# Pinning the high parts and squares of x tiles and of later tables on ScalarE, a later norm spread, and another product order for the last pair

## The chip, the cores and the metric

The kernel runs on one core of one Trainium2 chip. The metric is the device time of one execution in microseconds (us), lower being better; a measured time is the median of several runs. TensorE multiplies, ScalarE and VectorE work on its results and on its operands, GpSimd (POOL) and SyncE (SP) mostly issue DMAs.

## The reference

One decoder layer over x of shape (1, 2048, 1024) in float32, with 256 memory tokens:

```python
h = rmsnorm(x, mix_norm_g); proj = h @ w_in
q, k, v, g, u = split(proj)                    # five blocks of 512 columns
y_ret  = silu(g) * head_rmsnorm(retention(q, k, v, positions), ret_gn_g)   # 4 heads, rotary, chunks of 128
y_pool = pool_mixer(u, pool_w, pool_scale)     # windows 2, 4, 8, 16: mean minus token, a linear map per group
x = x + concat(y_ret, y_pool) @ w_out
x = x + cross_attn(rmsnorm(x, xa_norm_g), rmsnorm(mem, mem_norm_g), xa_wq, xa_wkv, xa_wo)   # 4 heads of 256
x = x + conv_glu_ffn(rmsnorm(x, ffn_norm_g), ...)   # causal width-3 convolution, silu(gate) * value, D_FF = 2816
return rmsnorm(x, final_norm_g)
```

## The kernel before

All activations stand transposed, channels on the 128 partitions and tokens along the free axis. The sequence is worked on in two halves of 1024 tokens (`b` = 0 and 1, `T` = 1024), each in two sub-halves of 512 (`SUB`). Every product is made of three passes with split operands: `split` writes a high part `hi` (ScalarE, L258, or L261 when a norm weight is multiplied in) and a low part `lo` = value minus `hi` (VectorE, L242 or L250), and `passes` issues hi x hi, hi x lo, lo x hi on TensorE (L266 to L268), 128x128 against 128x512. So almost every operand of TensorE is preceded by one ScalarE and one VectorE instruction.

The stages are: weights folded for the attention and x of the first half loaded (`folded_weights`, `load_x_wide`); for each half the values (`values`), the projections and retention, the output product with residual (`add_residual`), the cross-attention in folded form, and its output product; then the up and the down projections for both halves in `run`, with the sums of a Strassen-like scheme. GpSimd adds up sums of weight blocks in DRAM beside the first half (`weight_sums`), paced by a small ScalarE copy (L1027) and a GpSimd copy.

`attention(sums, beside, pace)` goes over 16 products of a 128-token row tile against a folded table, eight for the first pair of heads (`hp` = 0) and eight for the second (`hp` = 1). Each product is 24 matmuls. Behind it come row maximum, exponentials (ScalarE, L969), normalisation (VectorE, L246), and two products later the transposes of the probabilities (`turn`, TensorE L942, evacuated at L944). `load_m(hp)` fetches a table from DRAM (`Md`) in four pieces and splits it. The table of `hp` = 1 is fetched and split in the first four of the 16 steps.

After the attention of the first half come eight output units, one for each 128 channels (`unit` with `VWd`): 48 matmuls each, evacuated by `add_residual` onto `acc` with the square of the sum (L405 or L409), then stored (L2049). After each unit the program calls `load_x(n, nxt, got)`, which splits channel tile n of the second half of x into `X` and squares it for its norm, and then issues the fetch of the next one (`fetch_x`, L578). `X` is read by the attention's products until those end; the squares read only the fetched tile.

The generator `norms` then makes the factor of the second half's norm (`rows_norm`, narrow matmuls at L347), spreads it over the partitions (`spread_steps`: VectorE writes diagonals, TensorE multiplies them by ones at L398, ScalarE evacuates at L400), and makes the factor of the first half's own norm. It is advanced once for every 12 matmuls of `values`. Beside it `quarter_sums` combines x for the second half's projections (L1577, L1592 and VectorE), in program order already.

`head_projections` does the second half's projections as eight pairs of column blocks (`PAIRS`), each pair with seven products of 12 matmuls each on sums of the operands. Blocks 0 to 3 are q, 4 to 7 k, 8 to 11 the gates, 12 to 15 the pool groups of windows 2, 4, 8, 16. A block is complete when both of its sub-halves were evacuated the last time; a complete pool block queues `pool_steps` on VectorE, a complete q and k pair starts the head's retention (`kept`). Within the last pair these steps are queued behind the last head's factors (`chained`). `settle` splits finished parts into the operands of the output product, whose second half takes the parts in the order 2, 4, 5, 3 (4 is window 2, 5 is window 4). `scaled_tables` reads the rotary tables back from DRAM (`rope_d`) and multiplies them by the spread norm.

The order of the instructions on each engine is not that of the program. The kernel is written with

```python
with tile.TileContext(nc, schedule_with_timeline_sim=True) as tc:
```

and a planner places each instruction into its engine's queue by its own model of when the operands will be there; the queue is then run in that order. Three means set bounds to it: `tc.keep_in_program_order(ins)` puts an instruction behind the one that stands before it in the program on the same engine (and only behind that one); `tc.issue_after(ins)` puts the instructions of a block behind a given one on its engine; `tc.manual_schedule` fixes a stretch.

Of the kernel before, what the change touches and what calls it, by code (L numbers as in the profile page):

```python
# [11 lines left out]
AF = mybir.ActivationFunctionType  # L12
# [9 lines left out]
SUB = 512  # L22
# [8 lines left out]
EDGE = 16  # L31

ROUNDS = ((0, 3), (6, 4), (14, 4))
PAIRS = ((15, 8), (0, 4), (14, 9), (1, 5), (10, 11), (2, 6), (3, 7), (13, 12))

_PI = 314159265358979323846264338327950288419716939937510582097494459
_PI_DEN = 10**62
# [99 lines left out]
def trunk(ctx, tc, xT, memT, pos, w_qkgu, w_v, wkv, wqT, wo, wout_r, wout_p, poolT, w_up, w_dn, vecs, consts, outT):  # L137
    nc = tc.nc
    pe, act, dve, pool, sp = nc.tensor, nc.scalar, nc.vector, nc.gpsimd, nc.sync
# [37 lines left out]
    def vec(n):  # L177
        nonlocal o
        o += n
        return vc[:, o - n : o]  # L180

    mixg, xag, memg, ffng, fing = (vec(KT) for _ in range(5))
# [7 lines left out]
    def cst(n):  # L190
        nonlocal o
        o += n
        return cs_t[:, o - n : o]

    ident, one = cst(P), cst(1)
# [10 lines left out]
    Ud = drp.tile([NF, 4, P, SUB], F32, tag="Ud", name="Ud")  # L206
    Ad = drp.tile([len(PAIRS), 4, P, SUB], F32, tag="Ad", name="Ad")
    Dd = drp.tile([len(ROUNDS), KT // 2, 4, P, SUB], F32, tag="Dd", name="Dd")
# [23 lines left out]
    def aux():  # L232
        if both[0] and next(turns_) % 3 == 2:
            return single()
        return auxp.tile([P, SUB], F32, tag="aux", name=nm("aux"))

    def small(n=4):
        t = smp.tile([P, 8], F32, tag="sm", name=nm("sm"))
        return t[:, :n]

    def tt(eng, out, a, b, op):
        return eng.tensor_tensor(out=out, in0=a, in1=b, op=op)  # L242
# [6 lines left out]
    def stt(out, a, s, b, op0=ALU.mult, op1=ALU.add):  # L249
        dve.scalar_tensor_tensor(out=out, in0=a, scalar=s, in1=b, op0=op0, op1=op1)  # L250

    def bcast(v, n):
        return v.rearrange("p (a o) -> p a o", o=1).to_broadcast([P, v.shape[1], n])

    def split(src, hi, lo, g=None):

        if g is None:
            act.activation(hi, src, AF.Copy)  # L258
            tt(dve, lo, src, hi.bitcast(F32), ALU.subtract)
        else:  # L260
            act.activation(hi, src, AF.Identity, scale=g)  # L261
            stt(lo, src, g, hi.bitcast(F32), ALU.mult, ALU.subtract)

    def passes(ps, lhs, rhs, start, stop, more=False):
        (lh, ll), (rh, rl) = lhs, rhs
        pe.matmul(ps, lh, rh, start=start, stop=False, skip_group_check=more)  # L266
        pe.matmul(ps, lh, rl, start=False, stop=False, skip_group_check=more)  # L267
        latest[0] = pe.matmul(ps, ll, rh, start=False, stop=stop, skip_group_check=more)  # L268

    def new_raw():  # L270
        r = raws.take()
        r.free()
        return r.f
# [6 lines left out]
    def pairs(raw):  # L280

        out = []
        for h in range(2):
            r = raw[h] if isinstance(raw, list) else raw[:, h * SUB : (h + 1) * SUB]
            pr = new_pair()
            split(r, pr[:, 0], pr[:, 1])
            out.append(pr)
        return out
# [10 lines left out]
    def xpair(k, s):  # L299
        return X[:, 2 * k, s * SUB : (s + 1) * SUB], X[:, 2 * k + 1, s * SUB : (s + 1) * SUB]  # L300
# [79 lines left out]
    def spread_steps(y, outs):  # L380

        yh = smp.tile([P, 8], F32R, tag="yh", name=nm("yh"), bufs=1)[:, : y.shape[1]]
        yl = small(y.shape[1])
        dve.tensor_copy(yh, y)
        tt(dve, yl, y, yh.bitcast(F32), ALU.subtract)
        n, ds = SUB // P, []
        for s in range(len(outs)):
            ds.append(prs.take())
            for i, v in enumerate((yh.bitcast(F32), yl)):
                di = ds[s].r[:, i * SUB : (i + 1) * SUB]  # L390
                tt(dve, di.rearrange("p (a b) -> p a b", a=n), ident.rearrange("p (o b) -> p o b", o=1).to_broadcast([P, n, P]), bcast(v[:, s * n : (s + 1) * n], P), ALU.mult)
        yield
        yield
        for out, d in zip(outs, ds):
            ps = aux()
            with tc.issue_after(latest[0].ins):
                for i in range(2):
                    pe.matmul(ps, ones, d.r[:, i * SUB : (i + 1) * SUB], start=i == 0, stop=i == 1)  # L398
            d.free()
            act.activation(out, ps, AF.Copy)  # L400

    def squares(k, src, s_ap, eng=dve):

        if k == 0:
            act.activation(s_ap, src, AF.Square)  # L405
        else:
            q = TT.take()
            m = src.shape[-1]
            act.activation(q.f[:, :m], src, AF.Square)  # L409
            tt(eng, s_ap, s_ap, q.f[:, :m], ALU.add)  # L410
            q.free()


    def folded_weights():
# [166 lines left out]
    def load_x(k, s_acc, got):  # L581

        for s in range(NS):
            r = got[s].f[:, :SUB]
            split(r, *xpair(k, s), mixg[:, k : k + 1])
            squares(k, r, s_acc[s].f[:, :SUB])
            got[s].free()

    def load_x_wide(k, room):
# [324 lines left out]
    def attention(sums, beside, pace):  # L914
# [7 lines left out]
        def load_m(hp):  # L922

            out = mw[hp]
            for kp in range(KT // 2):
                raw = new_raw()
                fetched[0] = sp.dma_start(raw.rearrange("p (k n) -> p k n", k=2), Md[hp, 2 * kp : 2 * kp + 2].rearrange("k p n -> p k n"))
                if hp == 0 and kp == 0:

                    out += [(pr[:, 0], pr[:, 1]) for pr in pairs(raw)]  # L930
                    yield
                    continue
                for i in range(2):
                    u = tables[2 * hp].r[:, (2 * kp + i) * T : (2 * kp + i + 1) * T]
                    split(raw[:, i * SUB : (i + 1) * SUB], u[:, :SUB], u[:, SUB:])
                    out.append((u[:, :SUB], u[:, SUB:]))
                yield

# [11 lines left out]
        for _ in load_m(0):  # L950
            pass
        more_m = load_m(1)
        late = []
        for i in range(2 * KT):
            hp, t = divmod(i, KT)
# [4 lines left out]
            if i == 0:  # L960
                rn, _, _ = norm_tables(sums, wide=False)
# [35 lines left out]
    def weight_sums():  # L997

        jobs = [((w_qkgu[a], w_qkgu[c]), 0, 4, Ad[p]) for p, (a, c) in enumerate(PAIRS)]
        jobs += [((w_up[f], w_up[f + NF]), 0, 4, Ud[f]) for f in range(NF)]  # L1000
# [594 lines left out]
    def head_projections(b, v, rb, t1, t2, z):  # L1595
# [76 lines left out]
        class Heads(Member):  # L1672

            def __init__(self, p):
                super().__init__([w_qkgu[n] for n in PAIRS[p]], Ad[p], 0, 4)
                self.groups, self.how, self.seen, self.acc = PAIRS[p], [""] * 7, set(), None
                self.ended = []
# [87 lines left out]
            ready.append((h, outs[h]))  # L1765

        members = [Heads(p) for p in range(len(PAIRS))]
        items = [(m, i) for m in members for i in range(7)]
        fetches, made, highs = list(items), [], []

        def fetch():
# [147 lines left out]
    for b in range(NB):  # L1919
# [47 lines left out]
        if b:  # L1967
            first, order = 3, (6, 7, 0, 1, 2, 4, 5, 3)
            weights, evacs = [], []
            for n in range(first):  # L1970
                raw = new_raw()
                r = raw.rearrange("p (k c) -> p k c", c=P)
# [12 lines left out]
        for n in range(first, KT):  # L1985
            raw = new_raw()
# [215 lines left out]
```

## Time and profile before

| | |
|---|---|
| median of 3 runs | 2483.67 us (2480.16 to 2487.25) |
| profiled execution | 2483.87 us, span 2482.1 us |
| granted TensorE clock, mean | 0.993 |
| TensorE busy | 2418.8 us (97%) |
| VectorE busy | 1726.2 us (70%) |
| ScalarE busy | 1290.9 us (52%) |
| GpSimd busy | 319.5 us (13%) |
| read from and written to HBM | 398.65 MB, 187.43 MB |

Times inside the execution are in us from the start of its span. In a timeline a row is: start, duration, engine, source line, operation, destination <- sources by the program's names (buffer numbers left out), shape, count, and in brackets the idle time of the engine before it with what ended it. A line such as L242 is that of a helper, so the tile names tell the operations apart: `T` are temporaries, `Q`, `G`, `E`, `S`, `Z` operand buffers, `mm` and `aux` PSUM banks, `sm` small columns. "SPq" and "ACTq" are DMA issues from the queues of SyncE and ScalarE.

### The profile page before, as it was taken

What the parts mean: (1) busy time and instruction counts of PE and PEld (TensorE: products, weight loads), DVE (VectorE), ACT (ScalarE), POOL (GpSimd) and SP (SyncE); (2) the same over time, 40 slices, a digit from 0 to 9 for tenths busy, and PEclk for the clock granted to TensorE, in tenths of its full rate; (3) what the DMA queues carried; (4) which work ended last, traced back from release to release, by engine and by line L of the source; (5) the groups of instructions that cost most, each with busy time, mean ns of one, the idle gap of its engine ahead of it and who ended that gap; (6) DMA issues with size and microseconds to landing.
All of it is one profiled execution on the core that took longest, in us unless ns stands there. A gap on an engine that the chain in (4) does not pass through costs nothing.

```text
span 2482.1 us, 33252 instructions
## 1 busy us (share of the span) xinstructions
PE 2418.8 (97%) x11294; PEld 2018.0 (81%) x11294; DVE 1726.2 (70%) x2917; ACT 1290.9 (52%) x2349; POOL 319.5 (13%) x485
## 2 busy tenths in 40 slices
PE   6999999999999999999999999999999999999997
PEld 6888888877878887788888888888888887888886
DVE  8646576654666765575678876897667687867876
ACT  6333423443435553434655565665555576666663
POOL 1000000044255554200000010020000000000000
PEclk9999999999999999999999999999999999999998
DMA  7133524479799999757468665665456468758951
GB/s 285 50 111 111 159 75 136 140 192 324 211 299 267 278 225 318 204 187 253 146 195 274 215 189 159 219 219 170 160 157 216 134 225 294 248 187 280 344 173 68
DMA packets 263595, 502.35 MB, mean 202 GB/s; under 512 B 28800, under 2 KB 57600, under 8 KB 263424
## 3 DMA queue, kind: packets, MB, share of 16 engines
q1 hardware_dynamic: 201536, 385.90, 47.4%
q0 software_dynamic: 37376, 86.00, 14.7%
q10 hardware_dynamic: 24512, 28.32, 3.3%
q8 instruction: 89, 1.46, 0.2%
q14 instruction: 82, 0.67, 0.1%
HBM read 398.65 MB, written 187.43 MB: 236 GB/s over the span
## 4 chain that ended last, share of the span: by engine, by line
PE 87%; DMA 6%; DVE 4%; ACT 1%; issue 1%; SPq 0%; POOLq 0%; POOL 0%; DVEq 0%; ACTq 0%
PE mm L268 27%; PE mm L266 27%; PE mm L267 27%; DMA T<-xT 2%; DVE Z L242 1%; DMA S<-Md 1%; DVE G L242 1%; DMA rope_d<-T 1%; PE aux L820 1%; PE aux L793 1%; PE aux L804 1%; DVE T L242 1%; PE aux L266 1%; DVE Q L242 1%; PE aux L267 1%
## 5 line engine op out<-in xcount | busy, mean ns | idle before, releaser
L266 PE MATMUL mm<-G,Q 128*128 128x512 f32 (+1 forms) x1745 | 672.3, 386 | 17.3 <-ACT Q L258 11.5
L268 PE MATMUL mm<-G,Q 128*128 128x512 f32 (+1 forms) x1745 | 668.7, 385 | 13.3 <-DVE Q L242 13.2
L267 PE MATMUL mm<-G,Q 128*128 128x512 f32 (+1 forms) x1617 | 619.9, 384 | 0.0
L267 PE MATMUL mm<-G,E 128*128 128x512 f32 x1084 | 421.7, 389 | 0.0
L266 PE MATMUL mm<-G,E 128*128 128x512 f32 x1084 | 420.2, 390 | 0.0
L268 PE MATMUL mm<-G,E 128*128 128x512 f32 x1084 | 419.2, 389 | 0.0
L266 PEld LDWEIGHTS mm<-G,Q 128*128 128x128 f32 x1745 | 331.5, 190 | 82.4 <-ACT Q L258 13.0
L268 PEld LDWEIGHTS mm<-G,Q 128*128 128x128 f32 x1745 | 330.9, 190 | 79.1 <-DVE Q L242 16.1
L267 PEld LDWEIGHTS mm<-G,Q 128*128 128x128 f32 x1617 | 307.2, 190 | 56.4
L242 DVE TENSOR_TENSOR Z<-Z,mm 128x512 f32<-128x512 f32 x296 | 201.9, 683 | 105.5 <-PE mm L268 103.0
L250 DVE SCALAR_TENSOR_TENSOR Z<-Z,vecs 128x1024 f32<-128x1024 f32 x176 | 224.7, 1280 | 50.0 <-ACT Z L1177 45.4
L267 PEld LDWEIGHTS mm<-G,E 128*128 128x128 f32 x1084 | 203.5, 188 | 42.5 <-DVE G L242 0.4
L266 PEld LDWEIGHTS mm<-G,E 128*128 128x128 f32 x1084 | 203.4, 188 | 42.6 <-ACT G L1063 0.4
L268 PEld LDWEIGHTS mm<-G,E 128*128 128x128 f32 x1084 | 203.4, 188 | 42.4
L1114 ACT ACTIVATE E<-R 128x512 fp32r<-128x512 f32 (+1 forms) x165 | 101.5, 615 | 141.0 <-PE mm L267 132.1
L242 DVE TENSOR_TENSOR T<-T 128x512 f32<-128x512 f32 (+3 forms) x220 | 150.6, 690 | 21.3 <-ACT T L409 12.5
L242 DVE TENSOR_TENSOR Q<-R,Q 128x512 fp32r<-128x512 f32 x149 | 103.7, 699 | 77.2 <-ACT Q L258 54.9
L242 DVE TENSOR_TENSOR G<-T,G 128x512 fp32r<-128x512 f32 (+1 forms) x181 | 119.5, 675 | 43.7 <-ACT G L1063 32.0
L1114 ACT ACTIVATE Q<-R 128x512 fp32r<-128x512 f32 (+1 forms) x153 | 94.6, 618 | 87.1 <-PE mm L267 70.9
L1177 ACT ACTIVATE Z<-Z,vecs 128x1024 f32<-128x1024 f32 x88 | 109.1, 1241 | 37.6 <-DVE Z L242 36.7
L1063 ACT ACTIVATE G<-T 128x512 fp32r<-128x512 f32 x157 | 95.6, 624 | 54.7 <-DMA T<-Hd 27.2
L1114 ACT ACTIVATE E<-S 128x512 fp32r<-128x512 f32 (+1 forms) x107 | 65.8, 615 | 104.9 <-PE mm L267 101.3
(338 smaller groups left out, 3783.2 us busy)
## 6 DMA issues: line engine op xcount, KB each, us to landing
T<-Gd SPq DMA_DIRECT2D x168, 256.0 KB, 4.6
Ud<-w_up POOLq DMA_DIRECT2D x132, 256.0 KB, 10.3
Gd<-Z SPq DMA_DIRECT2D x110, 256.0 KB, 2.8
R<-Ud SPq DMA_DIRECT2D x106, 256.0 KB, 2.7
R<-w_up SPq DMA_DIRECT2D x80, 256.0 KB, 3.1
S<-Ud SPq DMA_DIRECT2D x70, 256.0 KB, 2.9
Gd<-T SPq DMA_DIRECT2D x56, 256.0 KB, 3.4
T<-Xd SPq DMA_DIRECT2D x53, 256.0 KB, 4.6
```

The costliest lines, as they stand in the source:

```text
L242: return eng.tensor_tensor(out=out, in0=a, in1=b, op=op)
L250: dve.scalar_tensor_tensor(out=out, in0=a, scalar=s, in1=b, op0=op0, op1=op1)
L266: pe.matmul(ps, lh, rh, start=start, stop=False, skip_group_check=more)
L267: pe.matmul(ps, lh, rl, start=False, stop=False, skip_group_check=more)
L268: latest[0] = pe.matmul(ps, ll, rh, start=False, stop=stop, skip_group_check=more)
L793: pe.matmul(col(sc, c), self.ch(k, c), self.ch(q, c), start=True, stop=True)
L804: pe.matmul(col(self.kv, c), col(self.kn.f, c), self.ch(v, c, h * T), start=True, stop=True)
L820: pe.matmul(col(y, c), col(self.pr.f, c), self.ch(v, c, h * T), start=True, stop=self.cur[c] is None)
L1063: act.activation(hi, x, AF.Copy)
L1114: act.activation(p2[:, 0, :w], self.raw[i].f[:, :w], AF.Copy)
L1177: act.activation(self.c[g].f, a[:, 2:], AF.Identity, bias=cb[:, f : f + 1], scale=cw[2][:, f : f + 1])
```

## The change

Four things are changed. `split` and `squares` take a flag `kept` with which their ScalarE instruction is put behind the previous ScalarE instruction of the program. It is set for the x tiles of the second half in `load_x` (all four ScalarE instructions of a tile) and in `load_m` for the table of the second pair of heads (`hp == 1`), in both halves. `spread_steps` gives control back six times instead of twice between writing the diagonals and multiplying them. In the last pair of column blocks the two blocks change places, (12, 13) for (13, 12), and its seven products run in the order 0, 2, 4, 6, 1, 3, 5.

```diff
-PAIRS = ((15, 8), (0, 4), (14, 9), (1, 5), (10, 11), (2, 6), (3, 7), (13, 12))
+PAIRS = ((15, 8), (0, 4), (14, 9), (1, 5), (10, 11), (2, 6), (3, 7), (12, 13))
...
-    def split(src, hi, lo, g=None):
+    def split(src, hi, lo, g=None, kept=False):
 
         if g is None:
-            act.activation(hi, src, AF.Copy)
+            one = act.activation(hi, src, AF.Copy)
             tt(dve, lo, src, hi.bitcast(F32), ALU.subtract)
         else:
-            act.activation(hi, src, AF.Identity, scale=g)
+            one = act.activation(hi, src, AF.Identity, scale=g)
             stt(lo, src, g, hi.bitcast(F32), ALU.mult, ALU.subtract)
+        if kept:
+            tc.keep_in_program_order(one)
...
-        yield
-        yield
+        for _ in range(6):
+            yield
...
-    def squares(k, src, s_ap, eng=dve):
+    def squares(k, src, s_ap, eng=dve, kept=False):
 
         if k == 0:
-            act.activation(s_ap, src, AF.Square)
+            one = act.activation(s_ap, src, AF.Square)
         else:
             q = TT.take()
             m = src.shape[-1]
-            act.activation(q.f[:, :m], src, AF.Square)
+            one = act.activation(q.f[:, :m], src, AF.Square)
             tt(eng, s_ap, s_ap, q.f[:, :m], ALU.add)
             q.free()
+        if kept:
+            tc.keep_in_program_order(one)
...
-            split(r, *xpair(k, s), mixg[:, k : k + 1])
-            squares(k, r, s_acc[s].f[:, :SUB])
+            split(r, *xpair(k, s), mixg[:, k : k + 1], kept=True)
+            squares(k, r, s_acc[s].f[:, :SUB], kept=True)
...
-                    split(raw[:, i * SUB : (i + 1) * SUB], u[:, :SUB], u[:, SUB:])
+                    split(raw[:, i * SUB : (i + 1) * SUB], u[:, :SUB], u[:, SUB:], kept=hp == 1)
...
-        items = [(m, i) for m in members for i in range(7)]
+        items = [(m, i) for m in members for i in ((0, 2, 4, 6, 1, 3, 5) if m is members[-1] else range(7))]
```

## The prediction

> **What bounds the kernel now.** I read the page first, then busy time by stretches, then the timelines of TensorE, ScalarE, VectorE and SyncE around every hole in TensorE's work.
>
> ```profile
> span 2482.1 us, 33252 instructions
> PE 2418.8 (97%) x11294; PEld 2018.0 (81%) x11294; DVE 1726.2 (70%) x2917; ACT 1290.9 (52%) x2349; POOL 319.5 (13%) x485
> ```
>
> TensorE is busy in 2418.8 of 2482.1 us. The profiled execution took 2483.9 us, 1.8 us over its span and 0.2 us over the median of the three runs (2483.7), so a sum made on its rows can be set against the median as it stands. No engine can save work here, because the change takes no matmul away; what it can win lies in the 63 us in which TensorE stood. The largest part of those lies in the first stage and at the end, which the change doesn't touch. The other holes lie in a few stretches:
>
> ```profile
> 505.00:545.00 40.00, 36.66 (x174) 30.03 (x173) 19.31 (x48) 18.35 (x42) 21.00 (x37) 1.00 0.86 217
> 545.00:590.00 45.00, 40.80 (x188) 33.45 (x187) 21.13 (x47) 17.08 (x47) 23.64 (x38) 0.96 1.07 276
> 590.00:664.00 74.00, 74.00 (x328) 61.28 (x327) 41.59 (x64) 32.56 (x55) 15.87 (x24) 1.00 0.88 268
> 664.00:735.00 71.00, 65.93 (x299) 54.32 (x298) 43.51 (x93) 28.80 (x55) 37.07 (x58) 0.98 1.01 277
> 900.00:960.00 60.00, 52.40 (x262) 42.43 (x261) 36.58 (x79) 22.45 (x59) 30.34 (x44) 0.97 0.90 238
> 1005.00:1040.00 35.00, 31.36 (x150) 25.88 (x150) 18.88 (x52) 12.96 (x31) 7.92 (x11) 1.00 0.97 249
> ```
>
> The columns are length, busy time (instructions) of TensorE, its weight loads, VectorE, ScalarE and GpSimd, the granted clock, the DMA share and GB/s. The stretch 590 to 664 shows TensorE without a hole: 74.00 us for 328 matmuls, 0.226 us each, which is the pace that I use below. The stretches beside it lost 3.34, 4.20, 5.07, 7.60 and 3.64 us, and three of them show a granted clock under 1.00. The first, second and last are the attention of the first and second half of the sequence. The timeline of ScalarE tells why, first for the first half:
>
> ```profile
> ...
> 530.62 0.63 ACT L405 ACTIVATE T<-T 128x512 f32<-128x512 f32 x1 [6.39 <-DMA T<-xT]
> 537.51 0.63 ACT L405 ACTIVATE T<-T 128x512 f32<-128x512 f32 x1 [6.26 <-DMA T<-xT]
> 538.61 0.56 ACT L969 ACTIVATE T<-mm,sm,scl 128x256 f32<-128x256 f32 x1
> ...
> 580.67 0.72 ACT L261 ACTIVATE G<-T,vecs 128x512 fp32r<-128x512 f32 x1 [4.28 <-DMA T<-xT]
> 581.81 0.55 ACT L969 ACTIVATE T<-mm,sm,scl 128x256 f32<-128x256 f32 x1
> ```
>
> L405 and L261 are the square and the high part of an x tile of the next half. They have nothing to do with the attention that runs here. The planner queued them ahead of the exponentials (L969), and ScalarE waited 6.39, 6.26 and, after a like wait, 4.28 us for their tiles, with the exponentials behind them. TensorE runs on until it needs the probabilities to transpose (L942):
>
> ```profile
> ...
> 540.54 0.63 PE L942 MATMUL aux<-consts,T 128*128 128x128 f32 x4 [3.34 <-DVE T L246]
> ...
> 583.73 1.09 PE L942 MATMUL aux<-consts,T 128*128 128x128 f32 x4 [4.20 <-DVE T L246]
> 584.47 0.78 PE L266 MATMUL mm<-G,Q 128*128 128x512 f32 x1
> ...
> 586.93 0.39 PE L266 MATMUL mm<-G,Q 128*128 128x512 f32 x1
> ```
>
> It stands 3.34 us and 4.20 us. After the second hole six matmuls, from 584.47 to 586.93, take 2.46 us in place of 6 x 0.226 = 1.36: another 1.1 us at the lower clock. For the second half the same thing is done by the high parts of the later table:
>
> ```profile
> ...
> 1017.18 1.15 ACT L258 ACTIVATE Z<-S 128x512 fp32r<-128x512 f32 x2 [5.55 <-DMA S<-Md]
> 1023.72 1.16 ACT L258 ACTIVATE Z<-S 128x512 fp32r<-128x512 f32 x2 [5.39 <-DMA S<-Md]
> 1029.10 1.28 ACT L969 ACT_TABLE_LOAD   x1 [4.22 <-DVE sm L246]
> ```
>
> ```profile
> ...
> 1025.60 0.16 DVE L247 TENSOR_SCALAR sm<-aux 128x8 f32<-128x8 f32 x1
> ```
>
> ```profile
> ...
> 1006.65 0.39 PE L266 MATMUL mm<-Q,G 128*128 128x512 f32 x1
> ...
> 1032.24 0.59 PE L942 MATMUL aux<-consts,T 128*128 128x128 f32 x3 [3.64 <-DVE T L246]
> ```
>
> The two Z<-S lines are the later table's, and wait 5.55 and 5.39 us for its DMA. VectorE's low parts follow them in its queue, so the sums of squares are taken up only at 1025.60, the first exponential's table load starts at 1029.10, and TensorE stands 3.64 us at 1032.24.
>
> **The change, part by part.** First, the pinned x tiles. Each high part and square is put behind ScalarE's previous instruction in the program, for the first of a tile the store of the finished residual (L2049). That store needs the output products of the same column tile, so no x tile can come before the attention's exponentials any more. This takes away both holes: 3.34 + 4.20 + 1.1 = 8.6 us. The instructions are the same ones, so nothing is added. The tile's DMA issues are not pinned, though the slots that they fill now come free later. What is late next is the exponentials' own chain. The stretches 505 to 545 and 545 to 590 lost 3.34 and 4.20 us in all, which is these two holes, so nothing else was late there, and I take nothing back.
>
> Where the tiles go now, they have cover if they have landed. An output unit is 48 matmuls, 48 x 0.226 = 10.8 us, and the fetch of the next tile is issued when the squares of one unit release their buffers:
>
> ```profile
> ...
> 631.89 3.66 SPq L578 DMA_DIRECT2D T<-xT  x2
> ```
>
> ```profile
> ...
> 642.18 0.72 ACT L261 ACTIVATE G<-T,vecs 128x512 fp32r<-128x512 f32 x1 [1.67 <-DMA T<-xT]
> ...
> 664.04 0.71 ACT L261 ACTIVATE G<-T,vecs 128x512 fp32r<-128x512 f32 x1
> ...
> 668.43 0.33 ACTq L2049 DMA_DIRECT2D Xd<-Z  x1
> 669.22 0.72 ACT L1577 ACTIVATE T<-S,vecs 128x512 f32<-128x512 f32 x1 [0.16 <-DVE T L242]
> ```
>
> The fetch issued at 631.89 was used at 642.18 by its second half, 10.3 us after the first issue, inside the 10.8 us that it has. The last tile changes its place most: its second high part ran at 664.04, and pinned it comes after the store at 668.43, with 0.71 us and a square of 0.63 us (L405 above) for each half, four instructions and about 2.7 us. The first instruction of the x sums (L1577, 669.22) is pinned in program order already, so it moves from 669.22 to some 671.5: 2.3 us later against TensorE. The value products start with this matmul:
>
> ```profile
> ...
> 664.47 0.39 PE L266 MATMUL mm<-G 128*128 128x512 f32 x1
> ```
>
> They need the last tile after 33 of them, 7.5 us later, at 672, which is about when its low part is there. I take no hole there, with 2 us as the bound.
>
> Second, the pinned tables. Their high parts now follow the exponentials of the first four row tiles. The DMA that came last was used at 1023.72, and the table is read only after eight products of 24 matmuls, 8 x 24 x 0.226 = 43 us after the first of them (1006.65), so these waits find cover: 3.64 us gone. In the first half the same pin moves eight high parts into a stretch without a hole; cover is the same 43 us, cost zero, and if VectorE should be late there it is the 2 us of its low parts.
>
> Third, the spread of the norm. Here TensorE waits for VectorE:
>
> ```profile
> ...
> 683.66 0.75 DVE L250 SCALAR_TENSOR_TENSOR Z<-S,vecs,T 128x512 f32<-128x512 f32 x1 [4.73 <-DMA S<-xT]
> ...
> 688.62 1.29 DVE L242 TENSOR_TENSOR Q<-consts,yh 128x512 fp32r<-128x512 f32 x2
> ```
>
> ```profile
> ...
> 689.36 0.80 PE L398 MATMUL aux<-Q,ones 128*128 128x512 f32 x1 [2.44 <-DVE Q L242]
> ...
> 692.48 0.39 PE L266 MATMUL mm<-E,G 128*128 128x512 f32 x1
> ```
>
> VectorE stood 4.73 us for an x tile in its queue, and the diagonals were written from 688.62 on; TensorE reached the first of the four spreading matmuls and stood 2.44 us. From 689.36 to 692.48 seven instructions take 3.12 us in place of 1.58: another 1.5 us at the lower clock. The generator is advanced once per 12 matmuls of the values. With six empty steps in place of two the spread is queued behind 108 of the 192 value matmuls at the earliest, not behind 60. From 664.47 that is 108 x 0.226 = 24.4 us, 688.9 without the narrow matmuls of the two norms between them, which make it later still; the first diagonal is written by 689.3. Gone: 2.44 + 1.5 = 3.9 us, but for a few tenths. What needs the spread norm, the scaled tables, waits longer for its DMA anyway:
>
> ```profile
> ...
> 726.58 1.29 DVE L242 TENSOR_TENSOR Z<-Z,T 128x512 f32<-128x512 f32 x2 [7.54 <-DMA Z<-rope_d]
> ```
>
> ```profile
> ...
> 730.92 0.50 PE L268 MATMUL mm<-G,Q 128*128 128x512 f32 x1 [2.63 <-DVE Q L242]
> ...
> 1116.48 0.63 PE L942 MATMUL aux<-consts,T 128*128 128x128 f32 x4 [1.31 <-DVE T L246]
> ```
>
> These are the two places that may take back what is won. At 726.58 VectorE has stood 7.54 us for the rotary tables, with the low part of a weight behind them, and TensorE stands 2.63 us at 730.92. That chain starts from the x sums and goes through DMAs; if it doesn't move with TensorE, the hole grows by up to the 3.9 us won just before and the 2.3 us of the later x sums. But by the program's order the last x sum is pinned behind an evacuation of the values, which comes earlier once TensorE no longer stands at 689.36. I take 2.0 us back, between 0 and 6.2. At 1116.48 the same transposes wait 1.31 us late in the second attention, where by the program ScalarE also takes in the first tiles of the next stage. Bounds: 0 and the 3.64 us won at 1032; I take 1.0 back, nearer to the lower end, since that work hangs on the attention's own progress.
>
> Fourth, the last pair. The order 0, 2, 4, 6, 1, 3, 5 and the swapped pair leave group 13 to be complete after the fifth product instead of the sixth, and group 12 after the last, as before. Both groups' pooling on VectorE stays queued behind the last head's factors. TensorE stands there because of that queue:
>
> ```profile
> ...
> 932.72 0.50 PE L268 MATMUL mm<-G,Q 128*128 128x512 f32 x1 [1.70 <-DVE Q L242]
> ...
> 935.32 1.65 PE L266 MATMUL mm<-E,Q 128*128 128x512 f32 x3 [1.87 <-ACT E L258]
> ```
>
> ```profile
> ...
> 934.64 0.63 ACT L258 ACTIVATE E<-Z 128x512 fp32r<-128x512 f32 x1 [3.83 <-DVE Z L250]
> ```
>
> It waits 1.70 us for a weight's low part and 1.87 us for a high part of the pooled group that the second half of the output product takes first. No instruction goes away; an evacuation of group 12 moves from ScalarE to VectorE. Bounds: the 3.57 us of these two rows as a gain, and as much as a loss. I take zero.
>
> Sum: won are 8.6 + 3.6 + 3.9 = 16.2 us before rounding, given back 2.0 + 1.0, which leaves -13.2 us, and 2483.9 - 13.2 = 2470.7 us.
>
> The lower clock is one place where the Trainium skill says otherwise. "TensorE: Matmul & The Clock Gate", section "HAM oscillation — how this bites in real kernels", gives as its rule that idle gaps beyond about 3.4 us are what bring the clock down. Here a hole of 2.44 us was followed by the slow stretch and holes of 3.34 and 3.64 us were not (granted clock 1.00 in 505 to 545 and in 1005 to 1040), so the trace differs and decides. By the rule the 1.5 us after the spread would not count, and the sum would be 2472.2 us.
>
> **The rivals.** One: given back. The holes close, but the chains behind them don't move: the rotary tables take 6.2 us back, the stretch at 1116 the full 3.64. Then the gain is 16.2 - 9.8 = 6.4 us: 2477.5 us. For it speaks that the DMA share is 1.01 in 664 to 735; against it that the chain leans on the values' evacuation. Chance 0.21.
>
> Two: slower. A pinned x tile holds the weights' high parts behind it. This decides if the tiles take longer than the 10.8 us of a unit to land. The chain has one that did:
>
> ```profile
> ...
> 935.84 15.74 DMA T<-xT
> ```
>
> At 15.74 us every unit from the third to the last would wait 15.74 - 10.8 = 4.9 us, since each fetch is issued only at a unit's end: six units, 29.6 us, less one 24-matmul half of split weights as cover, 5.4, and 4.9 more for the x sums at the seam: 29.1 us. With 16.2 won that gives 2483.9 - 16.2 + 29.1 = 2496.8 us. For it speaks the DMA share of 1.07 and 0.88 around these units; against it that the fetches there were used within 10.3 us. Beyond 24 us of such waits it turns the sign by more than 0.3%. Chance 0.13.
>
> Three: the pin doesn't hold what matters. It ties an instruction only to the one before it, and the planner may put another early instruction with a late DMA ahead of the exponentials; then only the spread's 3.9 us are won, 2480.0 us. Against it: in the rows only x tiles and tables stood there with waits over 4 us. Chance 0.06.
>
> **How the numbers follow.** The forecast has 0.60; 0.3% (7.4 us) is about what a measurement of this kernel can tell from no change, so below 2476.4 is faster. Faster: the forecast and 0.04 of the given-back case, where it gives back a little less, 0.64. Same: the rest of that case and rival three, 0.17 + 0.06 = 0.23. Slower: rival two, 0.13. The range: all holes closed with nothing given back and both waits of the last pair gone is 2483.9 - 16.2 - 3.6 = 2464.1; I go to 2463. At the other end it holds rivals one and three and the 2 to 6 us that the unknown costs could add to rival three, up to 2486.
>
> **What would show it.** Right: no L405 or L261 between the exponentials, no hole at 540, 584 or 1032 of TensorE's timeline, the spread without a wait, clock 1.00 in 545 to 590; at 731 a hole of 2 to 5 us. Wrong: holes in the output units with ScalarE waiting for T<-xT, a hole over 6 us before the rotary tables, or new holes where TensorE was full, after 1120.

## The result, and the profile after

The changed kernel takes 2466.31 us (median of 4 runs, 2464.59 to 2467.87) beside 2481.91 us for the kernel before (median of 4 runs): ratio 0.9935, 95% interval 0.9915 to 0.9954. The profiled execution took 2467.87 us, and its page begins:

```profile
span 2466.1 us, 33272 instructions
PE 2417.9 (98%) x11294; PEld 2019.7 (82%) x11294; DVE 1726.2 (70%) x2917; ACT 1288.9 (52%) x2349; POOL 316.1 (13%) x485
```

TensorE does the same 11294 matmuls in 2417.9 us instead of 2418.8; the span is 16.0 us shorter, so nearly all of it is time in which TensorE no longer stands. The same stretches as in the prediction (length, busy time and instructions of TensorE, weight loads, VectorE, ScalarE, GpSimd, granted clock, DMA share, GB/s; the events in them have moved by up to 15 us):

```profile
505.00:545.00 40.00, 40.00 (x191) 33.01 (x190) 22.21 (x55) 19.26 (x48) 24.52 (x40) 1.00 0.97 233
545.00:590.00 45.00, 45.00 (x212) 37.11 (x211) 20.83 (x41) 17.76 (x43) 21.48 (x35) 1.00 1.07 294
590.00:664.00 74.00, 74.00 (x336) 61.59 (x335) 50.98 (x81) 37.09 (x64) 18.87 (x31) 1.00 0.90 277
664.00:735.00 71.00, 64.20 (x270) 52.26 (x269) 40.15 (x87) 23.97 (x46) 37.88 (x60) 0.93 1.03 280
900.00:960.00 60.00, 56.94 (x272) 46.01 (x271) 39.40 (x83) 23.15 (x62) 29.67 (x49) 1.00 0.94 262
1005.00:1040.00 35.00, 35.00 (x174) 29.18 (x173) 21.59 (x62) 16.32 (x43) 4.37 (x6) 1.00 0.73 181
```

Both attentions are full now, at clock 1.00. The seam between them, 664 to 735 (values, spread and first head products), is worse than before: 64.20 us busy, 6.80 us of holes instead of 5.07, and a granted clock of 0.93 instead of 0.98. The last pair's stretch, 900 to 960, which was forecast unchanged, lost 7.60 us before and loses 3.06 now. TensorE's timeline says the same at the events (start, duration, line, operation; in brackets the idle time before it and what ended it; L946 are the transposes, L400 the spread, L268 to L270 the three passes):

```profile
535.03 0.60 PE L946 MATMUL aux<-consts,T 128*128 128x128 f32 x4
...
571.59 0.38 PE L946 MATMUL aux<-consts,T 128*128 128x128 f32 x2
...
679.56 0.85 PE L400 MATMUL aux<-Q,ones 128*128 128x512 f32 x3
...
704.34 0.68 PE L268 MATMUL mm<-G,Q 128*128 128x512 f32 x1 [2.76 <-ACT Q L1118]
...
707.80 0.44 PE L268 MATMUL mm<-G,Q 128*128 128x512 f32 x1
...
718.90 0.80 PE L270 MATMUL mm<-G,Q 128*128 128x512 f32 x1 [4.03 <-DVE Q L242]
...
725.02 0.39 PE L269 MATMUL mm<-G,Q 128*128 128x512 f32 x1
...
924.99 0.50 PE L270 MATMUL mm<-G,Q 128*128 128x512 f32 x1 [0.59 <-DVE Q L242]
...
926.99 0.96 PE L268 MATMUL mm<-E,Q 128*128 128x512 f32 x3 [1.27 <-ACT E L258]
...
1018.93 0.60 PE L946 MATMUL aux<-consts,T 128*128 128x128 f32 x4
...
1101.63 0.63 PE L946 MATMUL aux<-consts,T 128*128 128x128 f32 x4 [1.72 <-DVE T L246]
```

The transposes that waited 3.34, 4.20 and 3.64 us and the spread that waited 2.44 us have no bracket any more. Two holes stand in the seam instead, at the first products of the heads. Each is followed by matmuls at the lower clock: eight from 704.34 take 3.46 us in place of 8 x 0.226 = 1.81, and fourteen from 718.90 take 6.12 in place of 3.16. With the holes that is 2.76 + 1.65 + 4.03 + 2.96 = 11.4 us. Before, one hole of 2.63 us stood in their place, without any lower clock behind it. So 8.8 us are given back at the first head products.

What held the two products is seen on ScalarE and on VectorE. ScalarE first:

```profile
681.41 0.72 ACT L1581 ACTIVATE T<-R,vecs 128x512 f32<-128x512 f32 x1
691.51 0.63 ACT L1118 ACTIVATE S<-R 128x512 fp32r<-128x512 f32 x1 [9.38 <-DMA R<-w_qkgu]
...
694.58 0.73 ACT L261 ACTIVATE G<-R,vecs 128x512 fp32r<-128x512 f32 x1 [1.86 <-DVE R L242]
...
698.76 0.63 ACT L1118 ACTIVATE Q<-R 128x512 fp32r<-128x512 f32 x1 [2.00 <-DMA R<-Ad]
```

L1581 begins the last x sum, L261 goes on with it. Between them the planner now put L1118, the high part of a head weight whose transfer had only been issued at 682.93. ScalarE stood 9.38 us for it. The x sum behind it kept its buffers meanwhile, and three of the next weights, whose high parts the first head products need, were fetched only from 696.12 on; that the one follows from the other is tested by the first move below. On VectorE it is the rotary tables:

```profile
714.83 1.29 DVE L242 TENSOR_TENSOR Z<-Z,T 128x512 f32<-128x512 f32 x2 [8.69 <-DMA Z<-rope_d]
716.95 1.29 DVE L242 TENSOR_TENSOR Z<-Z,T 128x512 f32<-128x512 f32 x2 [0.83 <-DMA Z<-rope_d]
718.16 0.68 DVE L242 TENSOR_TENSOR Q<-S,Q 128x512 fp32r<-128x512 f32 x1
```

Q<-S is the low part of a weight, and TensorE waited for it at 718.90; it stood in the queue behind four multiplications of the rotary tables (two in each row above it), for whose transfers VectorE waited 8.69 and 0.83 us.

### The profile page after: what moved, and what is told of

Its sections match the earlier page's. It is cut to its first block, busy times and chain, and to the rows that moved or that the text cites. A ratio compares the mean times of both kernels' runs of the same rounds, so it can differ in the third digit from the quotient of the medians.

```text
span 2466.1 us, 33272 instructions
## 1 busy us (share of the span) xinstructions
PE 2417.9 (98%) x11294; PEld 2019.7 (82%) x11294; DVE 1726.2 (70%) x2917; ACT 1288.9 (52%) x2349; POOL 316.1 (13%) x485
## 4 chain that ended last, share of the span: by engine, by line
PE 93%; DMA 3%; DVE 3%; issue 1%; ACT 0%; SPq 0%; POOL 0%; POOLq 0%; DVEq 0%; ACTq 0%
PE mm L270 29%; PE mm L268 29%; PE mm L269 29%; DMA T<-Xd 1%; PE aux L808 1%; PE aux L824 1%; PE aux L797 1%; PE aux L268 1%; PE aux L269 1%; PE aux L270 1%; PE aux L826 1%; PE aux L349 1%; DMA Z<-rope_d 1%; DMA T<-xT 0%; DVE T L242 0%
## 5 line engine op out<-in xcount | busy, mean ns | idle before, releaser
L268 PE MATMUL mm<-G,Q 128*128 128x512 f32 (+1 forms) x1745 | 673.4, 386 | 19.8 <-ACT Q L258 11.0
L270 PE MATMUL mm<-G,Q 128*128 128x512 f32 (+1 forms) x1745 | 669.9, 385 | 10.5 <-DVE Q L242 10.4
L268 PE MATMUL mm<-G,E 128*128 128x512 f32 x1084 | 420.1, 390 | 0.0
L270 PE MATMUL mm<-G,E 128*128 128x512 f32 x1084 | 419.2, 389 | 0.0
L268 PEld LDWEIGHTS mm<-G,Q 128*128 128x128 f32 x1745 | 332.0, 190 | 84.8 <-ACT Q L258 12.4
L270 PEld LDWEIGHTS mm<-G,Q 128*128 128x128 f32 x1745 | 331.5, 190 | 76.0 <-DVE Q L242 13.2
L270 PEld LDWEIGHTS mm<-G,E 128*128 128x128 f32 x1084 | 203.5, 188 | 42.4
L268 PEld LDWEIGHTS mm<-G,E 128*128 128x128 f32 x1084 | 203.5, 188 | 42.1 <-ACT Z L1263 0.2
L1118 ACT ACTIVATE E<-R 128x512 fp32r<-128x512 f32 (+1 forms) x165 | 101.5, 615 | 142.3 <-PE mm L269 135.1
L1118 ACT ACTIVATE Q<-R 128x512 fp32r<-128x512 f32 (+1 forms) x153 | 94.5, 618 | 85.4 <-PE mm L269 72.2
L1067 ACT ACTIVATE G<-T 128x512 fp32r<-128x512 f32 x157 | 95.7, 624 | 58.1 <-DMA T<-Hd 27.9
L1118 ACT ACTIVATE E<-S 128x512 fp32r<-128x512 f32 (+1 forms) x107 | 65.8, 616 | 105.0 <-PE mm L269 103.4
```

What stands on the lines that cost most here:

```text
L1067: act.activation(hi, x, AF.Copy)
L1118: act.activation(p2[:, 0, :w], self.raw[i].f[:, :w], AF.Copy)
```

## The experiments

Two theories were open. The prediction's: the change is a sum of parts, each worth the hole that it closes. Its rival: each edit makes the planner order the other instructions anew, so a part's worth depends on its company. I ran each part alone on the kernel before, then the whole change without one part, and then two moves at the seam that undo what held TensorE there. Gains in us are (1 - ratio) x 2482 us; the interval of most ratios is about 0.0015 to each side, 3 to 4 us. The kernel before took 2481.8 to 2485.3 us beside the different groups of runs, so ratios are compared, and medians only where the kernels before agree. Each trace is one execution of its kernel, and the executions of one kernel spread by 2 to 14 us, so the traces show which waits there are and not a part's worth to the microsecond.

**Each part alone, on the kernel before.** The x tiles:

```
-            split(r, *xpair(k, s), mixg[:, k : k + 1])
-            squares(k, r, s_acc[s].f[:, :SUB])
+            split(r, *xpair(k, s), mixg[:, k : k + 1], kept=True)
+            squares(k, r, s_acc[s].f[:, :SUB], kept=True)
```

> Only the x tiles are pinned; tables, spread and last pair are as before. Theory (the holes add up part by part): the holes of 3.34 and 4.20 us in the first attention go, with the 1.1 us of lower clock, so 8.6 us are won by the prediction's sum, up to 10.1 us by what the two traces show between the 9th and the 16th transposes: 2472 to 2473.5 us where the kernel before takes 2481.9; the 2.44 us hole before the spread stays. Rival (the seam takes it back): the x sums come later behind the pinned last tile, the hole before the heads grows by 2 to 6 us, and 2475 to 2479 us are left.

Measured: 2467.82 us, ratio 0.9927 (0.9914 to 0.9941), 18.1 us won, more than both theories gave and no less than the whole change. The holes at 540 and 584 are gone, and the seam paid something too. TensorE's timeline of this kernel, whose spread comes after two empty steps as before:

```profile
680.90 0.39 PE L400 MATMUL aux<-Q,ones 128*128 128x512 f32 x1
...
716.50 0.50 PE L270 MATMUL mm<-G,Q 128*128 128x512 f32 x1 [1.38 <-DVE Q L242]
...
1019.16 0.70 PE L946 MATMUL aux<-consts,T 128*128 128x128 f32 x4 [3.18 <-DVE T L246]
```

The spread has no wait. With the x tiles pinned the planner put it behind 96 value matmuls instead of 82, 14 x 0.226 = 3.2 us later, and VectorE's diagonals came 1.1 us earlier after the first value matmul. So the spread's 3.9 us come with the pinned x tiles here. In the traces the spans differ by 13.9 us; this profiled execution was the slowest of its six (2469.93 us), and the other 4 us of the ratio aren't placed.

The tables (`kept=hp == 1` in the tables' split), alone:

> Only the later tables' high parts are pinned. Theory: the hole of 3.64 us before the second attention's first transposes goes and nothing is late next, 2478.3 us (before: 2481.9). Rival one: the transposes that wait 1.31 us at 1116 take it back, 2481.9 us. Rival two: the 2 us that the whole change gained in the start-up comes with any edit, since the plan is made anew: then 2476.3 us, and the first attention's transposes are 2 us early here too.

Measured: 2476.06 us, ratio 0.9973 (0.9962 to 0.9983), 6.7 us. The hole at 1032 is gone and the transposes that waited 1.31 us wait 1.43, so rival one falls. The 3 us above the theory aren't the start-up's, where only 0.6 us are won. Every kernel here has the same 11294 matmuls, so the start times of the same matmul can be compared in two traces. By them this kernel gains in two places that its edit doesn't touch: 2.5 us at the seam and 2.4 us after 1245 us. At the seam the spread hardly waits any more, though the x tiles aren't pinned here. It still stands behind 82 value matmuls, but VectorE writes the diagonals 2.3 us sooner after the first of them than in the kernel before:

```profile
687.14 0.50 PE L400 MATMUL aux<-Q,ones 128*128 128x512 f32 x1 [0.17 <-DVE Q L242]
```

Whether the plan or the transfers of that one execution did this isn't known. After 1245 the whole change and the other three parts gain too (1.5 to 2.5 us). The kernel before has holes of 0.69 and 0.40 us there, at 2099 and 2104, which hardly any new plan has; what the rest of the gain is isn't placed. The last 20 us take up to 1.3 us of it back, so a part measured alone contains 0.3 to 2.5 us from these stages.

The later spread (`for _ in range(6): yield` in place of two), alone:

> Only the spread of the norm is later. Theory: 2.44 us of hole and 1.5 us of lower clock go, and the rotary tables take 0 to 2 us back: 2478 to 2480 us (before: 2481.9). Rival: the chain from the x sums through the weights' and the rotary tables' transfers sets the first head products, so the hole there grows by the whole 3.9 us and the time stays at 2481.9 us; the whole change shows holes of 2.76 and 4.03 us there.

Measured: 2484.01 us, ratio 1.0002 (0.9990 to 1.0014): nothing, as the rival says. The spread has no wait, but the first head product waits 2.09 us at 715.71 for a weight's high part, where it didn't wait before, and 2.79 us at 727.41. By the start times of the same matmuls the spread wins 4.1 us, and by 760 us 3.7 of them are lost again.

The last pair (the two edits of PAIRS and the order of its products), alone:

> Only the last pair is changed (groups 12 and 13 exchanged, products in the order 0, 2, 4, 6, 1, 3, 5). Theory of the prediction: nothing is won, 2481.9 us, since VectorE's queue and not the order sets the two waits there. Rival, from the two traces: TensorE's holes between 920 and 955 us go from 7.5 us in all to 2.6, so 4 to 5 us are won by this edit alone, 2477 to 2478 us. If the holes stay as before here, the gain came from another part of the change, through the plan.

Measured: 2481.07 us, ratio 0.9984 (0.9975 to 0.9992), 4.0 us: the rival. The two waits at the end of the stretch are

```profile
927.48 0.50 PE L268 MATMUL mm<-G,Q 128*128 128x512 f32 x1 [0.59 <-DVE Q L242]
...
929.48 0.81 PE L266 MATMUL mm<-E,Q 128*128 128x512 f32 x2 [1.27 <-ACT E L258]
```

0.59 and 1.27 us instead of 1.70 and 1.87; the same numbers stand in the whole change. The third wait of before isn't there either. In the kernel before it is, on VectorE and then on TensorE:

```profile
951.67 0.69 DVE L242 TENSOR_TENSOR T<-T,mm 128x512 f32<-128x512 f32 x1 [2.25 <-DMA T<-xT]
952.28 0.68 DVE L242 TENSOR_TENSOR Q<-S,Q 128x512 fp32r<-128x512 f32 x1
```

```profile
953.02 0.50 PE L268 MATMUL mm<-G,Q 128*128 128x512 f32 x1 [2.56 <-DVE Q L242]
```

This wait has a cause of its own: VectorE waits for an x tile of the residual (the transfer of 15.74 us in the prediction's second rival), with a weight's low part behind it. With the tables' pin alone, without the pair's edits, it is 0.95 us (at 949.82). So what surely belongs to the pair are the first two waits. This profiled execution was the fastest of its twelve (2474.49 us); it is read for its stretch, not for its span.

**The whole change without one part.** Without the later spread:

> The changed kernel with the spread of the norm back at two empty steps; pins and last pair stay. Theory (the later spread costs at the seam): with the x tiles pinned alone the spread already had no wait, and the second half's last transposes of retention came 14.4 us earlier than before, with the whole change only 7.3; so this wins about 7 us more, 2459 to 2461 us where the changed kernel takes 2466.3. Rival (the prediction's): the hole of 2.44 us with 1.5 us of lower clock comes back before the spread, 2470 us.

Measured: 2459.82 us (2457.09 to 2461.68), ratio 0.9914 (0.9898 to 0.9931), 21.3 us won, 5.2 more than the whole change by the ratios; the intervals of the two ratios overlap, but the runs don't, beside kernels before of 2481.8 and 2481.9 us. This version beats both kernels. Its profiled execution was the fastest of its six and the changed kernel's the slowest of its four, so their traces lie further apart (10.8 us) than the two kernels do. ScalarE at the same place of this kernel:

```profile
679.73 0.72 ACT L1581 ACTIVATE T<-R,vecs 128x512 f32<-128x512 f32 x1
680.54 1.30 ACT L402 ACTIVATE T<-aux 128x512 f32<-128x512 f32 x2
681.84 0.72 ACT L261 ACTIVATE G<-R,vecs 128x512 fp32r<-128x512 f32 x1
...
689.04 0.63 ACT L1118 ACTIVATE S<-R 128x512 fp32r<-128x512 f32 x1 [5.12 <-DMA R<-w_qkgu]
```

The last x sum goes on at 681.84 instead of 694.58, and the weight's high part waits behind it. The stretch 650 to 735, of the kernel before, the changed kernel and this one:

```profile
650.00:735.00 85.00, 79.93 (x361) 65.93 (x360) 53.64 (x108) 37.69 (x71) 37.07 (x58) 0.98 0.93 259
```

```profile
650.00:735.00 85.00, 78.20 (x339) 64.14 (x339) 53.90 (x110) 31.07 (x60) 42.17 (x65) 0.94 0.98 269
```

```profile
650.00:735.00 85.00, 84.54 (x388) 69.95 (x387) 59.05 (x118) 37.67 (x71) 42.17 (x66) 1.00 1.01 284
```

TensorE is busy in 84.54 of 85 us, at full clock. On TensorE the spread itself hardly moved: it stands 25.5 us after the first value matmul here (96 value matmuls and 32 narrow ones) and 26.3 us in the changed kernel (108 and 16). What the six empty steps changed is the order of what stands around it.

Without the changed last pair:

> The changed kernel with the last pair as before; pins and later spread stay. Theory (the pair's order earns what its stretch shows): the holes between 920 and 955 us are 7.5 us again in place of 2.6, 2470 to 2471 us where the changed kernel takes 2466.3. Rival (prediction: worth nothing; what the pair alone gained came from the plan made anew): 2466 us within 2.

Measured: 2471.47 us, ratio 0.9958 (0.9943 to 0.9974). It costs 5.7 us against the whole change by the ratios, about what the theory says, and the old waits are back:

```profile
924.85 0.50 PE L270 MATMUL mm<-G,Q 128*128 128x512 f32 x1 [1.72 <-DVE Q L242]
...
927.45 0.80 PE L268 MATMUL mm<-E,Q 128*128 128x512 f32 x1 [1.87 <-ACT E L258]
...
944.65 0.50 PE L270 MATMUL mm<-G,Q 128*128 128x512 f32 x1 [2.44 <-DVE Q L242]
```

The last pair's two edits apart, on the better version, with only the order of the products kept:

```
-PAIRS = (... (3, 7), (12, 13))
+PAIRS = (... (3, 7), (13, 12))
```

> The version without the later spread, with the last pair's products in the new order but its groups as before, 13 first and 12 second, so that group 12 is complete after the fifth product and group 13 only after the last. Theory (the order alone frees VectorE): the holes between 910 and 945 us stay at some 3.8 us, and 2459.8 us where the kernel before takes 2481.8, a ratio of 0.9914. Rival (the exchange is needed, since group 13 has one step of pooling more than group 12 and would now come last): the holes are 7.5 us or more, 2465 us or more, a ratio of 0.9935 or above.

Measured: 2461.14 us, ratio 0.9914 (0.9898 to 0.9930), the same as with the exchanged groups: the theory, and below the rival's 0.9935 with the whole interval. TensorE's holes of 0.4 us and more in that stretch are two, 4.7 us together, 0.9 us more than the theory's 3.8:

```profile
914.13 0.50 PE L268 MATMUL mm<-G,Q 128*128 128x512 f32 x1 [0.49 <-ACT Q L258]
...
932.20 0.50 PE L268 MATMUL mm<-G,Q 128*128 128x512 f32 x1 [4.18 <-ACT Q L258]
```

The two waits for the pooled groups and their weight are gone altogether. The other wait is longer than the 1.45 us that the version with both edits has at that place. It is again the residual's x tile, for which VectorE waits 5.61 us at 926.58 here. Within the interval, the order earns what the pair earns.

Without the tables' pin, and on the better version, so x tiles and last pair alone:

> The x tiles pinned and the last pair changed; tables and spread as before. Theory (the tables' pin is worth its hole): the hole of 3.2 to 4.1 us before the second attention's first transposes is there, 2463 to 2464 us beside 2459.8 for the same kernel with the tables pinned. Rival: the tables' pin is worth the 6.7 us that it won alone, through the plan, 2466.5 us.

Measured: 2465.84 us, ratio 0.9924 (0.9910 to 0.9938), by the ratio 2.5 us less won than with the tables pinned. The intervals overlap, so the time alone settles nothing; the trace has the hole back at the second attention's first transposes, and no other of that size between the start-up and the last microseconds:

```profile
1015.06 0.69 PE L946 MATMUL aux<-consts,T 128*128 128x128 f32 x2 [3.60 <-DVE T L246]
```

Without the pinned x tiles:

> The changed kernel without the pinned x tiles; tables, later spread and last pair stay. Theory (holes by place): the holes at 540 and 584 come back, some 8.6 to 10 us with the lower clock, and the seam keeps two holes: 2475 to 2476 us (changed kernel: 2466.3). Rival one (the parts' own times add up): tables 6.7, spread 0 and pair 4.0 us won alone, 2471 us. Rival two: the pinned x tiles are worth in company the 17 to 18 us that they were worth alone, 2483 us.

Measured: 2475.70 us, ratio 0.9963 (0.9949 to 0.9978), 9.2 us won. The x tiles are worth 6.9 us in this company, not 18: rival two falls; between the theory and rival one the time (2472.8 us by the ratio) can't choose. The trace shows the theory's holes, smaller:

```profile
538.13 0.52 PE L946 MATMUL aux<-consts,T 128*128 128x128 f32 x3 [1.48 <-DVE T L246]
...
580.35 0.66 PE L946 MATMUL aux<-consts,T 128*128 128x128 f32 x2 [3.24 <-DVE T L246]
...
713.21 0.75 PE L268 MATMUL mm<-G,Q 128*128 128x512 f32 x1 [2.90 <-ACT Q L1118]
```

**Two moves at the seam of the changed kernel.** Neither touches the spread. The first puts the first four head weights' high parts behind the last x sum on ScalarE (last_sum is that sum's last instruction there):

```
+                with tc.issue_after(last_sum.ins) if len(made) < 5 else nullcontext():
                     highs.append((m, i, *m.high(i, made[-1])))
```

> The changed kernel, with the first four head weights' high parts queued behind the last x sum on ScalarE. Theory: the high part that waited 9.4 us for its weight held the last x sum, and through it the buffers and the transfers of the next weights; without it the hole of 2.76 us at 704 and some 1.9 us of lower clock go, and the rotary tables are fetched earlier: 2461 us or less (changed kernel: 2466.3). Rival: the transfers of the weights themselves set the first head product; the hole moves and stays, 2466 us.

Measured: 2461.85 us, ratio 0.9923 (0.9908 to 0.9939). By the medians that is the theory's 4.5 us, by the ratios 3.0, with intervals that overlap. The trace settles it: the hole at 704 is gone, the first head product comes without a wait, and the same matmul starts 4 us sooner at that place. The rotary tables' hole is left, 3.59 us at 717.24. So the high part in front of the x sum was the cause of the first hole.

The second move puts the tables' multiplication behind a later weight's low part on VectorE:

```
+                    with tc.issue_after(lowered[-3].ins):
                         tt(dve, d, d, rb[s].f[:, :SUB], ALU.mult)
```

> The changed kernel, with the multiplication of the rotary tables queued behind the low part of a later head weight on VectorE. Theory: the tables' transfer, for which VectorE stood 8.7 us, no longer holds the low parts behind it, and the hole of 4.03 us at 719 goes with some 3.0 us of lower clock: 2459 to 2460 us (changed kernel: 2466.3). Rival: the weight for the product after it waits 6.5 us for its own transfer on ScalarE, so TensorE stands nearly as long at the next product, 2464 to 2466 us.

Measured: 2463.86 us, ratio 0.9928 (0.9914 to 0.9943), 2.5 us better than the changed kernel by the medians and 1.7 by the ratios: just below the rival's range, and far from the theory's 2459 to 2460. The hole of 4.03 us is gone, and the next products wait 1.40 us at 721.12 and 1.54 us at 731.84. Both together:

> The changed kernel with both moves at the seam: the first head weights' high parts behind the last x sum on ScalarE, and the rotary tables' multiplication behind a later low part on VectorE. Theory: with the first move alone one hole of 3.59 us was left at 717, held by the multiplication; it goes with its lower clock, 2456 to 2458 us. Rival: the weight of the next product waits for its own transfer, and the time stays at the 2461.9 us of the first move alone.

Measured: 2463.01 us, ratio 0.9912 (0.9895 to 0.9929). By the ratio it is as good as the version without the later spread, and not to be told from the first move alone. Its trace shows the rival's wait, first on TensorE, then on ScalarE:

```profile
719.91 0.50 PE L268 MATMUL mm<-G,S 128*128 128x512 f32 x1 [2.73 <-ACT S L1120]
```

```profile
719.23 0.63 ACT L1120 ACTIVATE S<-R 128x512 fp32r<-128x512 f32 x1 [8.95 <-DMA R<-w_qkgu]
```

With the multiplication out of the way the next weight's own transfer is late. Beside the first move alone, 3.59 - 2.73 = 0.9 us of the second hole went.

## Why the prediction was right, and where it was not

The forecast of 2470.7 us stood 4.4 us above the median of 2466.3, and the sign and the size were right. The sum behind it was right only in part, and two of its errors cancel.

**Pinned x tiles, 8.6 us.** Right in mechanism and place: both holes are gone, the clock in 545 to 590 is 1.00, and what was late next was nothing. The tiles found the cover that was argued. ScalarE does wait for one of them, with the weights behind it,

```profile
605.35 0.72 ACT L261 ACTIVATE G<-T,vecs 128x512 fp32r<-128x512 f32 x1 [4.96 <-DMA T<-xT]
```

but TensorE was full from 590 to 664, so rival two (slower) didn't come about. What the step missed is that the pin also moves the spread: without any other edit that hole is closed too.

**Pinned tables, 3.6 us.** Right: no hole at 1018.93, and 3.60 us of hole again without the pin.

**Later spread, 3.9 us.** The hole is gone, but the pinned x tiles close it without the later spread, the pinned tables alone leave 0.17 us of it and the last pair alone 0.91 us, and in the company of the rest the later spread costs 5.2 us. The step that failed is the count "108 in place of 60": 60 was the earliest place, and the planner had put the spread behind 82 matmuls before and, with the x tiles pinned, behind 96. I had costed a moved step on the assumption that its neighbours stay.

**Given back at the rotary tables, 2.0 us, between 0 and 6.2.** Mis-sized, and outside its bounds: 8.8 us. The chain was the right one (x sums, transfers of weights and tables, VectorE's queue), and the hole that was forecast at 731 with 2 to 5 us came at 718.90 with 4.03. But the bounds took TensorE's shift as the worst case. They left out that ScalarE's order could change in front of the chain, which was the 9.38 us wait for a weight, and that the two holes bring 1.65 + 2.96 = 4.6 us of lower clock.

**At 1116, 1.0 us.** 1.72 instead of 1.31 us, so 0.4 us, within its bounds. Its cause is of the same kind as that of the holes at 540 and 584. ScalarE has a first tile of the next stage (L1067) ahead of the exponentials (L973 here) and waits 6.43 us for it, 6.02 us before the change:

```profile
1099.17 0.63 ACT L1067 ACTIVATE G<-T 128x512 fp32r<-128x512 f32 x1 [6.43 <-DMA T<-Hd]
1099.71 0.55 ACT L973 ACTIVATE T<-mm,sm,scl 128x256 f32<-128x256 f32 x1
```

No edit touches these tiles, and no run here pins them.

**Last pair, 0 us within 3.57.** The failing term on the other side: the holes of 920 to 955 went from 7.5 us to 3.0, which is 4.5 us, and six matmuls from 935.32 that took 2.73 us in place of 1.36 run at full pace, another 1.4 us. Alone the edit wins 4.0 us. I argued that VectorE's queue and not the order sets these waits; the runs show that the two that I named go and come back with the order. The order alone is enough. That one group, whichever it is, is then complete after the fifth product and its pooling out of VectorE's way sooner fits this, but is argued. The bound was too small because it left out the lower clock and the third wait, 2.56 us at 953. I had shown the transfer behind that wait, 15.74 us from 935.84, without seeing that a hole ends it; it is the residual's, and that it went isn't shown to be the order's doing.

**Not in the sum:** 2.0 us before the first attention's holes, half of them in the start-up, which between these kernels move by -2.0 to +0.6 us without an edit there; 2.4 us after 1245, of which the last 20 us take 1.3 back; a new hole of 1.05 us at 882. By the start times of the same matmuls the whole adds up: 2.0 us won before 530, 9.2 at the first two holes, 4.1 at the spread, 8.6 lost at the first head products, 4.6 won from there to 960, 3.9 at the tables, 0.4 lost at 1116, 2.4 won after 1245 and 1.3 lost at the end are 15.9 us, where the spans differ by 16.0. So the forecast was close partly by luck: 6 us too little were taken back, and 7.7 us were won in places that it had at zero.

Rival one (given back, 6.4 us left) had the right mechanism at the rotary tables, and even too small a price there; the last pair and the stages without an edit made up for it. Rival three fell as it was put: the holes at 540, 584 and 1032 are closed. Its kind is there at 1101 as it was before, where the prediction knew of x tiles and tables alone with waits over 4 us, and it came true at the seam, where an instruction with a late transfer was put ahead of the last x sum.

## What to carry to other kernels

In a kernel whose order a planner makes, an edit's worth isn't the hole that it closes: the parts won 18.1, 6.7, -0.5 and 4.0 us alone, 28.3 together, and 16.1 in company. One reason shows in the traces: the hole of 2.44 us before the spread goes or shrinks with every one of the four, so it is counted four times, and so is the gain after 1245. Look at each engine for instructions that wait for a transfer, ask what stands behind them, and pin that work ahead of them rather than move the step at which the hole shows. And take a part out again when the rest is in: the later spread answered a hole that the pinned x tiles had already closed.

## What the hardware showed

The length of a hole doesn't say whether the lower clock follows, or when. Before, 2.44 us at 689 brought it and 2.63 us at 731 didn't; in the changed kernel 2.76 us at 704 did. The kernel with the first move has 3.59 us, and then full pace for 1.6 us before the slow stretch begins:

```profile
717.24 0.50 PE L270 MATMUL mm<-G,Q 128*128 128x512 f32 x1 [3.59 <-DVE Q L242]
717.58 0.39 PE L268 MATMUL mm<-G,Q 128*128 128x512 f32 x1
...
718.88 0.63 PE L270 MATMUL mm<-G,Q 128*128 128x512 f32 x1
...
721.86 0.44 PE L268 MATMUL mm<-G,S 128*128 128x512 f32 x1
```

From 718.88 to 721.86 seven matmuls stand 0.43 us apart, nearly twice 0.226. The Trainium skill, "TensorE: Matmul & The Clock Gate", section "Part 1: The HAM clock gate (the "warmup" mystery)", says that the clock is judged over windows of 3413 ns that run freely and don't restart with the kernel, and that it is low after at least one idle window. The late onset agrees with windows that don't start with the hole; that a whole idle window is needed doesn't agree with the holes of 2.44 and 2.76 us. In a sum like the prediction's the lower clock should stand as a term of its own: the seam's 6.8 us of holes cost 4.6 us more by it. In the version without the later spread no slow stretch is left between the start-up and the last 20 us (mean granted clock 0.996, the changed kernel's 0.992).
